# Later places for retention values, operand halves, squares and residual loads in a one-core decoder trunk

## The chip, the cores and the metric

The kernel runs on one core of a Trainium2 chip. Its five engines work side by side and wait for each other by semaphores: TensorE (PE, matmuls into PSUM), VectorE (DVE), ScalarE (ACT), GpSimd (POOL) and SyncE (SP, which here only issues transfers). The metric is the device time of one execution in microseconds (us); lower is better.

## The reference

One layer of a decoder trunk on 16 + 256 tokens of width 2048, in float32:

```python
u = rmsnorm(h, attn_norm) * vmask
aq, ak, av, rq, rk, rv, rg = split(u @ w_in)
ya = rmsnorm(diff_attention(aq, ak, av, lam, slopes, valid), attn_subln) * (1 - lam_init)
yr = rmsnorm(retention(rq, rk, rv, log_g), ret_norm) * silu(rg)
h = h + concat([ya, yr]) @ w_out
u = rmsnorm(h, ffn_norm) * vmask
h = h + (silu(causal_conv3(u @ w_gate)) * (u @ w_up)) @ w_down
out = rmsnorm(h, final_norm)[:, CHUNK:]
```

There are 8 attention heads (each with two 64-wide halves of q and k, whose softmaxes are subtracted) and 4 retention heads (128-wide q and k, 256-wide v, a decay matrix in the place of the softmax).

## The kernel before

**Precision.** Each float32 operand is split into a high part (`whi`, `xhi`, `fhi`: a cast on ACT) and a low part (`wlo`, `xlo`, `flo`: source minus high part, on DVE). A product takes three matmuls: high by high, high by low, low by high.

**Weights.** All weights stream from HBM in chunks of 128x2048 (1 MB, `raw`), loaded by `load` on SP's queue. Each chunk gives two halves of 128x1024, split by `prep`, whose inner function `halves` issues the cast and the subtraction (lines 204 and 205). `ahead(hf)` issues loads some halves ahead and splits two halves ahead (three in the last stage).

**Stages.** First the input projection, 48 units: each `gemm` (lines 434 to 436) runs 16 k-steps of three matmuls into one PSUM tile. Units 0 to 23 are q, k, v of the eight attention heads; then come q, k and two v units of each retention head and two gate units each, in the order `RSEQ`. Then the output projection (16 units), gate and up projections (88 units), and the down projection.

**The side queue.** All else in the first stages is put as small tasks into the list `side`. `pump(n)` runs n of them, every fourth k-step, so a place of the list is 4 x 3 = 12 matmuls. `att_tasks` gives an attention head's tasks (scores, softmax, transposes, values), `ret_tasks` a retention head's: `scores`, `vtr` (loads the transposed values `rvt` back from DRAM), five empty places, `av` (the value matmuls, line 619, into `ro`), an empty place, `stats`, `scale`. The values get there by `turned`: a DVE transpose to `rvb`, four small transfers to DRAM (`rhv`), and two back (`rvt`, lines 609 and 610). A scheduler orders the instructions of each engine by these places and by its own estimate of when inputs are ready; calls under `keep` hold their order.

**Halves of q and k.** After an attention head's three units, lines 682 to 691 issue at once, for each half, two casts on ACT and three DVE operations: the low part of q into `q2`, a copy of k into `k2`, and the low part of k into `klz`.

**Down.** `down_order` lays out two groups g = 0, 1, each of two 512-wide column blocks for two row blocks (four results `o`) and helper sums (`x`). A group's entries are 20 plain ones (`w`: 12 matmuls, one split) and 12 times four parts of a Strassen-like product (`d`, `u`, `t`, `c`: 6, 6, 6 and 3 matmuls, four splits and one more subtraction). `LEAD[g]` sets how many plain entries open and close it; the others are spread between the parts. The last `HOLD` = 6 entries of group 1 are held for the very end. When a group's last part is done, side tasks join the helper sums to the residual (`joined`), add the results (`take`), and square and weigh them for the final norm (`finish`: a square on ACT, line 878, and a product with the norm's weights on DVE, line 884). The residual `htok` comes back from DRAM by two loads on SP's queue at entries 20 and 28 of group 0 (line 977).

Of the kernel before, what the change touches and what calls it, by code (L numbers as in the profile page):

```python
# [2 lines left out]

# [1 line left out]

# [5 lines left out]
F32 = mybir.dt.float32  # L11
# [4 lines left out]
ALU = mybir.AluOpType  # L16
# [30 lines left out]
NS = 12  # L47
KP = 2 * NS
NPL = (NF - KP) // 2
LEAD = [(4, 3), (0, HOLD + 3)]  # L50
PARTS = ("d", "u", "t", "c")
ROOMS = (0, 1, "2a", "2b", "3a", "3b")
RSEQ = [("y", 0), ("g", 0), ("y", 1), ("g", 1), ("y", 2), ("y", 3), ("g", 2), ("g", 3)]
# [62 lines left out]
def trunk_kernel(ctx, tc, a, out):  # L116
# [73 lines left out]
    def prep(hf):  # L190
        c, s = entries[hf]
        held = len(entries) - 1 - hf
        if held < 2:
            hi, lo = [big.tile([P, 1024], F32R, tag=f"act{2 + held}{i}", name=f"end{held}{i}")
                      for i in "ab"]
        elif c >= nw and (hf - 2 * nw) % 4 == 3:
            wx = big.tile([P, 2 * 1024], F32R, tag="act0", name=f"wx{hf}")
            hi, lo = wx[:, :1024], wx[:, 1024:]
        else:
            hi = wp.tile([P, 1024], F32R, tag="whi", bufs=3, name=f"whi{hf}")  # L200
            lo = wp.tile([P, 1024], F32R, tag="wlo", bufs=3, name=f"wlo{hf}")

        def halves(src, b, e):
            S.copy(out=hi[:, b:e], in_=src)  # L204
            V.tensor_tensor(out=lo[:, b:e], in0=src, in1=hi[:, b:e].bitcast(F32),  # L205
                            op=ALU.subtract)

        if c in mixed:
            g, p = divmod(mixed[c], NS)
            if s == "d":  # L210
                halves(raw[c][:, :2 * NW], 0, 2 * NW)
            elif s == "u":
                halves(raw[c][:, 2 * NW:], 0, 2 * NW)
                two = raw[c][:, :2 * NW].rearrange("p (a c) -> p a c", a=2)
                t2 = raw[c][:, 2 * NW:3 * NW].unsqueeze(1).to_broadcast([P, 2, NW])
                V.tensor_tensor(out=two, in0=two, in1=t2, op=ALU.subtract)
            elif s == "t":
                halves(raw[c][:, :2 * NW], 0, 2 * NW)
            else:
                halves(pools["sw"][g, p], 0, NW)  # L220
        else:
            halves(raw[c][:, s * 1024:(s + 1) * 1024], 0, 1024)
        pairs[hf] = (hi, lo)
        if s in (1, PARTS[-1]):
            raw.pop(c)
# [234 lines left out]
    with ExitStack() as p1:  # L460
# [27 lines left out]
                    out=hv[:, d:d + 32].rearrange("(b t) f -> t b f", t=32),  # L488
                    in_=vb[i * 32:(i + 1) * 32].rearrange("t (b f) -> t b f", f=32))

        def att_tasks(h, q, k, hv):
            slope = 2.0 ** (-(h + 1))
            tasks = []
            As = {}
# [1 line left out]
            at = [ap_.tile([P, 3 - j, QT], F32, tag=f"at{j}", name=f"at{h}_{j}")  # L496
                  for j in range(3)]
            bias = ap_.tile([QT, 3, T], F32, tag="bias", bufs=1, name=f"bias{h}")

            def prelude():  # L500
                S.activation(out=bias, in_=base, func=AF.Copy, scale=slope)
# [76 lines left out]
            def values():  # L578
                av()
                while late:  # L580
                    late.pop()()
                late.append(ytr)

            return [prelude, scores(0), scores(1), nop, scores(2), vload, nop, atr,
                    nop, values, nop, nop]

        def ret_tasks(r, k, q, hv):
            dt_ = ap_.tile([P, 2, NQ], F32, tag="t", name=f"dk_{r}")
# [56 lines left out]
                    V.tensor_tensor(out=t, in0=st["y"][:, c, :NQ], in1=st["r"], op=ALU.mult)  # L645
                    yn[r, c] = t

            return [scores, vtr, nop, nop, nop, nop, nop, av, nop, stats, scale]

        yn = {}  # L650

# [12 lines left out]
        for h in range(AH):  # L664
            q = ap_.tile([P, NQ], F32, tag="q", name=f"q{h}")
            k = ap_.tile([P, T], F32, tag="k", name=f"k{h}")
            v = ap_.tile([P, TV], F32, tag="v", name=f"v{h}")
            nc.gpsimd.memset(v[:, T:], 0.0)
            ps = gemm(idx, xhi, xlo, Q0, NQ, 1)
            V.scalar_tensor_tensor(out=q, in0=ps[:, :NQ], scalar=0.125, in1=rq_,  # L670
                                   op0=ALU.mult, op1=ALU.mult)
            ps = gemm(idx + 1, xhi, xlo, 0, T, 1)
            V.tensor_tensor(out=k, in0=ps[:, :T], in1=rk_, op=ALU.mult)
            ps = gemm(idx + 2, xhi, xlo, 0, T, 1)
            V.tensor_tensor(out=v[:, :T], in0=ps[:, :T], in1=rk_, op=ALU.mult)
            hv = dp.tile([TV, P], F32, name=f"hv{h}")
            turned(v, ap_.tile([P, TV], F32, tag="g0", name=f"vb{h}"), hv, 0)
            idx += 3
            q2 = ap_.tile([P, 2, NQ], F32R, tag="q2", name=f"q2_{h}")
            k2 = ap_.tile([P, 2, T], F32R, tag="k2", name=f"k2_{h}")  # L680
            kl = klz[:, h % 2]
            for m in range(2):
                hs, os = slice(m * 64, m * 64 + 64), slice(64 - m * 64, 128 - m * 64)
                S.copy(out=q2[hs, m], in_=q[hs])
                V.tensor_tensor(out=q2[os, m], in0=q[hs], in1=q2[hs, m].bitcast(F32),
                                op=ALU.subtract)
                S.copy(out=k2[hs, m], in_=k[hs])
                V.tensor_copy(out=k2[os, m], in_=k[hs])
                V.tensor_tensor(out=kl[hs, m], in0=k[hs], in1=k2[hs, m].bitcast(F32),
                                op=ALU.subtract)  # L690
            side.extend(att_tasks(h, q2, (k2, kl), hv))
        for kind, r in RSEQ:
            if kind == "g":
                for c in range(2):
# [59 lines left out]
    with ExitStack() as p2:  # L754
# [156 lines left out]
        for g in range(2):  # L911
# [60 lines left out]
            held = []  # L972
            for i, (kind, x, y) in enumerate(seq):
                ahead(e)
                if not g and i in (20, 28):
                    m = (i - 20) // 8
                    keep(nc.sync.dma_start(out=htok[:, m], in_=hd[m * P:(m + 1) * P]))
                if g and i >= len(seq) - HOLD:
                    held.append((y, e))
                    e += 1  # L980
                    continue
                wt = pairs[e]
                if kind == "w":
                    for m in range(2):
                        for kk in range(2):
                            product((m, x % 2), acts(m, KP + 2 * y + kk), wt, kk * NW)
                elif y == "d":
                    product((0, 0), acts(0, 2 * x + 1), wt, 0)
                    product((0, 1), forms(x, 2), wt, NW)
                elif y == "u":  # L990
                    product(6, forms(x, 0), wt, 0)
                    product(7, forms(x, 1), wt, NW)
                elif y == "t":
                    product((1, 0), acts(1, 2 * x + 1), wt, 0)
                    product(5, acts(1, 2 * x), wt, NW)
                else:
                    product(1, acts(0, 2 * x), wt, 0)
                pairs.pop(e)
                e += 1
                if i == last_s:  # L1000
                    side.extend(joined())
                    side.extend([take(0, 0), finish(0, 0), take(1, 0), finish(1, 0)])
                    if g:
                        side.append(lambda: S.activation(out=root, in_=so[:, 1, 2:3],
                                                         func=AF.Sqrt))
                pump(3 if i > last_s else 1)
            pump(len(side))
            if not g:
                take(0, 1)()
                take(1, 1)()  # L1010
                side.extend([finish(0, 1), finish(1, 1), lambda: norm(1)])
                side.extend([nop] * 12 + [lambda: norm_scale(1)])
                continue
            po = [bank[0, 1], bank[1, 1]]
# [117 lines left out]
```

## Time and profile before

| | us |
|---|---|
| median of three runs (1162.79 to 1163.71) | 1163.69 |
| the profiled execution | 1163.84 |
| its span, first to last instruction | 1162.0 |
| TensorE busy in the span | 1144.7 |
| TensorE idle in 250 to 300 us (second and third retention head) | 4.56 |
| TensorE idle in 1150 to 1162 us (end) | 7.91 |

An instruction row of the profile has its start, its duration, the engine, the line, the operation and what it writes and reads. In brackets stands how long the engine was idle before it and what ended that. A row of the list of waits has engine, line and what was waited for, then the total in us, the number of waits and the longest. A window row has the stretch and, for each engine, its busy time and count in that stretch, then the granted clock of TensorE, the share of the DMA engines and GB/s. Matmuls are pipelined: the durations of neighbours overlap, and what a matmul costs is the distance between two starts.

### The profile page before, as it was taken

The numbers are of one execution on the slowest core, as the hardware profiler recorded it, in microseconds if no ns is written. First come the engines' busy times: TensorE is split into PE (matmuls) and PEld (weight loads), VectorE is DVE, ScalarE is ACT, GpSimd is POOL, SyncE is SP. The second block draws the span as 40 slices with busy tenths as digits, with TensorE's granted clock in tenths as the row PEclk, the third lists the DMA queues.
The fourth block names the chain that finished last, engine by engine and source line by source line (L and its number), as shares of the span: only waits on it lengthen the run. The fifth ranks groups of instructions, "written<-read, shape, count | busy, mean of one in ns | idle before, by whom it ended". The sixth has DMA issues, their size and how long they took to land.

```text
span 1162.0 us, 20666 instructions
## 1 busy us (share of the span) xinstructions
PE 1144.7 (99%) x7967; PEld 1069.8 (92%) x7967; DVE 931.5 (80%) x1737; ACT 604.0 (52%) x996; POOL 36.2 (3%) x84
## 2 busy tenths in 40 slices
PE   9999999989999999999999999999999999999997
PEld 8999999989999999999999999999999988887886
DVE  7888887657577778888888888788787778899896
ACT  7566665433245444545444544444444455666663
POOL 0000000000000000000000000000000000000000
PEclk9999999999999999999999999999999999999999
DMA  8544545564547776776777677787786589869871
GB/s 306 200 165 159 168 153 189 172 212 156 159 166 235 230 228 207 254 272 240 270 283 257 246 278 267 274 299 267 278 281 238 210 297 373 287 251 333 299 283 72
DMA packets 94914, 276.37 MB, mean 238 GB/s; under 512 B 43490, under 2 KB 51082, under 8 KB 73056
## 3 DMA queue, kind: packets, MB, share of 16 engines
q1 hardware_dynamic: 86512, 237.69, 59.3%
q0 software_dynamic: 8160, 37.23, 8.6%
q8 instruction: 62, 1.02, 0.3%
q14 instruction: 36, 0.29, 0.1%
q10 hardware_dynamic: 144, 0.14, 0.1%
HBM read 251.17 MB, written 23.86 MB: 237 GB/s over the span
## 4 chain that ended last, share of the span: by engine, by line
PE 92%; DMA 5%; DVE 2%; issue 0%; SPq 0%; ACT 0%; DVEq 0%; ACTq 0%
PE mm L455 14%; PE mm L444 10%; PE mm L442 10%; PE mm L443 10%; PE mm L457 7%; PE mm L435 7%; PE mm L434 7%; PE mm L436 7%; PE o L857 4%; PE o L858 4%; PE o L859 4%; PE x L857 2%; PE x L859 2%; PE x L858 2%; DMA rvt<-rhv 1%; DMA raw<-in_w_first_dram 1%
## 5 line engine op out<-in xcount | busy, mean ns | idle before, releaser
L204 ACT CAST whi<-raw 128x1024 fp32r<-128x1024 f32 x381 | 399.3, 1051 | 381.1 <-issue 86.7
L205 DVE TENSOR_TENSOR wlo<-raw,whi 128x1024 fp32r<-128x1024 f32 x381 | 464.7, 1223 | 139.0 <-ACT whi L204 133.8
L455 PE MATMUL mm<-g,whi 128*128 128x512 f32 x352 | 124.4, 393 | 0.0
L434 PE MATMUL mm<-x,whi 128*128 128x272 f32 (+1 forms) x344 | 101.0, 293 | 0.0
L436 PE MATMUL mm<-x,wlo 128*128 128x272 f32 (+1 forms) x344 | 99.6, 290 | 1.2 <-DVE wlo L205 1.2
L435 PE MATMUL mm<-x,whi 128*128 128x272 f32 (+1 forms) x344 | 100.0, 291 | 0.0
L444 PE MATMUL mm<-g,wlo 128*128 128x258 f32 x352 | 99.5, 283 | 0.0
L442 PE MATMUL mm<-g,whi 128*128 128x260 f32 x352 | 99.3, 282 | 0.0
L457 PE MATMUL mm<-g,wlo 128*128 128x256 f32 x352 | 98.7, 280 | 0.0
L443 PE MATMUL mm<-g,whi 128*128 128x256 f32 x352 | 97.9, 278 | 0.0
L455 PEld LDWEIGHTS mm<-g,whi 128*128 128x128 f32 x352 | 66.1, 188 | 13.0
L442 PE MATMUL mm<-ys,whi 128*128 128x260 f32 x256 | 71.9, 282 | 0.0
L444 PE MATMUL mm<-ys,wlo 128*128 128x258 f32 x256 | 71.9, 281 | 0.0
L443 PE MATMUL mm<-ys,whi 128*128 128x256 f32 x256 | 70.8, 277 | 0.0
L443 PEld LDWEIGHTS mm<-g,whi 128*128 128x128 f32 x352 | 66.7, 190 | 1.9
L436 PEld LDWEIGHTS mm<-x,wlo 128*128 128x128 f32 x344 | 65.7, 191 | 1.4 <-DVE wlo L205 1.4
L457 PEld LDWEIGHTS mm<-g,wlo 128*128 128x128 f32 x352 | 66.3, 188 | 0.0
L442 PEld LDWEIGHTS mm<-g,whi 128*128 128x128 f32 x352 | 66.1, 188 | 0.0
L444 PEld LDWEIGHTS mm<-g,wlo 128*128 128x128 f32 x352 | 66.1, 188 | 0.0
L435 PEld LDWEIGHTS mm<-x,whi 128*128 128x128 f32 x344 | 65.8, 191 | 0.1
L434 PEld LDWEIGHTS mm<-x,whi 128*128 128x128 f32 x344 | 65.8, 191 | 0.1
L858 PE MATMUL o<-wlo,fhi 128*128 128x512 f32 x158 | 61.9, 391 | 0.1
(404 smaller groups left out, 3063.2 us busy)
## 6 DMA issues: line engine op xcount, KB each, us to landing
raw<-in_w_in_dram SPq DMA_DIRECT2D x44, 1024.0 KB
raw<-in_w_gate_dram SPq DMA_DIRECT2D x44, 1024.0 KB
raw<-in_w_up_dram SPq DMA_DIRECT2D x44, 1024.0 KB
raw<-in_w_down_dram SPq DMA_DIRECT2D x20, 1024.0 KB
ts<-in_w_mix_dram POOLq DMA_DIRECT2D x24, 768.0 KB, 5.9
raw<-in_w_out_dram SPq DMA_DIRECT2D x16, 1024.0 KB
td<-ts POOLq DMA_DIRECT2D x24, 512.0 KB, 4.5
raw<-in_w_mix_dram SPq DMA_DIRECT2D x24, 512.0 KB
```

The source lines that it names most:

```text
L204: S.copy(out=hi[:, b:e], in_=src)
L205: V.tensor_tensor(out=lo[:, b:e], in0=src, in1=hi[:, b:e].bitcast(F32), op=ALU.subtract)
L434: PE.matmul(ps[:, :n], wh, xh, start=(k == 0), stop=False)
L435: PE.matmul(ps[:, :n], wh, xl, start=False, stop=False)
L436: PE.matmul(ps[:, :n], wl, xh, start=False, stop=(k == KT - 1))
L442: PE.matmul(ps[:, :NQ + 2], wh, src.cols(k, GO - 2, GL), start=(k == 0), stop=False)
L443: PE.matmul(ps[:, 4:NQ + 2], wh, src.cols(k, GL, GW), start=False, stop=False)
L444: PE.matmul(ps[:, 2:NQ + 2], wl, src.hi(k), start=False, stop=(k == KT - 1))
L455: PE.matmul(ps, wh, src.cols(k, GO + 2, GW), start=(k == 0), stop=(k == KT - 1))
L457: PE.matmul(ps[:, :SEQ], wl, src.cols(k, GO + 2, GL), start=False, stop=False)
L857: PE.matmul(o, ah, wh, start=start, stop=False)
L858: PE.matmul(o, ah, wl, start=False, stop=False)
```

## The change

The value matmuls of retention heads 0 to 2 stand two places later in the side queue (`av`, and with it `stats` and `scale`); head 3 keeps its places. The halves of q and k become a task of their own, `parted`, at the head of an attention head's list, one place after the head's units; one empty place at the list's end goes. Within it the DVE operations of one half now stand together, and for heads 0 and 1 they are kept in order. The splits of halves 9 to 15 are issued with high priority. In down, group 1 opens with two plain entries instead of none and closes with one less; the squares and weighings of group 0's first column block move from that group's end into group 1, with those of the second block; the residual loads go from entries 20 and 28 to 40 and 48.

```diff
-LEAD = [(4, 3), (0, HOLD + 3)]
+LEAD = [(4, 3), (2, HOLD + 2)]
 def halves(src, b, e):
-    S.copy(out=hi[:, b:e], in_=src)
-    V.tensor_tensor(out=lo[:, b:e], in0=src, in1=hi[:, b:e].bitcast(F32),
-                    op=ALU.subtract)
+    with tc.high_priority() if 8 < hf < 16 else nullcontext():
+        S.copy(out=hi[:, b:e], in_=src)
+        V.tensor_tensor(out=lo[:, b:e], in0=src, in1=hi[:, b:e].bitcast(F32),
+                        op=ALU.subtract)
...
+def parted():
+    pin = keep if h < 2 else (lambda ins: ins)
+    for m in range(2):
+        hs, os = slice(m * 64, m * 64 + 64), slice(64 - m * 64, 128 - m * 64)
+        S.copy(out=q[hs, m], in_=qf[hs])
+        pin(V.tensor_tensor(out=q[os, m], in0=qf[hs], in1=q[hs, m].bitcast(F32),
+                            op=ALU.subtract))
+        S.copy(out=k[0][hs, m], in_=kf[hs])
+        pin(V.tensor_copy(out=k[0][os, m], in_=kf[hs]))
+        pin(V.tensor_tensor(out=k[1][hs, m], in0=kf[hs],
+                            in1=k[0][hs, m].bitcast(F32), op=ALU.subtract))
...
-return [prelude, scores(0), scores(1), nop, scores(2), vload, nop, atr,
-        nop, values, nop, nop]
+return [parted, prelude, scores(0), scores(1), nop, scores(2), vload, nop, atr,
+        nop, values, nop]
...
-return [scores, vtr, nop, nop, nop, nop, nop, av, nop, stats, scale]
+return [scores, vtr, *[nop] * (7 if r < RH - 1 else 5), av, nop, stats, scale]
...
-if not g and i in (20, 28):
-    m = (i - 20) // 8
+if not g and i in (40, 48):
+    m = (i - 40) // 8
     keep(nc.sync.dma_start(out=htok[:, m], in_=hd[m * P:(m + 1) * P]))
...
 if i == last_s:
     side.extend(joined())
-    side.extend([take(0, 0), finish(0, 0), take(1, 0), finish(1, 0)])
+    side.extend([take(0, 0), take(1, 0)])
     if g:
+        side.extend([finish(0, 0), finish(1, 0)])
         side.append(lambda: S.activation(out=root, in_=so[:, 1, 2:3], func=AF.Sqrt))
...
 if not g:
     take(0, 1)()
     take(1, 1)()
-    side.extend([finish(0, 1), finish(1, 1), lambda: norm(1)])
+    side.extend([finish(m, j) for m, j in ((0, 0), (1, 0), (0, 1), (1, 1))])
+    side.append(lambda: norm(1))
```

The instructions of an engine stand as follows (numbers behind names are buffers; the changed program's lines are shifted by 1 to 13). TensorE at the second retention head's values, before; `mm` is the first unit of the third head, `ro` the values, `sd` the decayed scores:

```order
L436 MATMUL mm_3636<-x_69,wlo_3566 128x272
L619 MATMUL ro_3621<-sd_0_3485,rvt_3488 128x258
L434 MATMUL mm_3636<-x_69,whi_3565 128x272
L435 MATMUL mm_3636<-x_70,whi_3565 128x272
L619 MATMUL ro_3621<-sd_1_3486,rvt_3488 128x172
L619 MATMUL ro_3621<-sd_2_3487,rvt_3488 128x86
```

and with the change, at the end of the same unit's first eight k-steps:

```order
L436 MATMUL mm_3625<-x_70,whi_3565 128x272
L437 MATMUL mm_3625<-x_69,wlo_3566 128x272
L632 MATMUL ro_3656<-sd_0_3485,rvt_3488 128x258
L632 MATMUL ro_3656<-sd_1_3486,rvt_3488 128x172
L632 MATMUL ro_3656<-sd_2_3487,rvt_3488 128x86
```

The same three come once more, for the other half of the values, before the unit goes on.
From this head's score matmuls to its first value matmul stand 93 unit matmuls before and 108 now; for the first head it is 58 and 82, for the third 84 and 108, for the last 84 and 84. The two unit matmuls that stood inside the group are gone from it.

VectorE after the first four units, before; `q`, `k`, `v` with `mm` are the units' results taken from PSUM, `q_0`, `k_0`, `klz` the halves of the first head, `q_1`, `k_1` of the second, `wlo_656` and `wlo_719` low halves of the weights of units 6 and 7:

```order
L685 TENSOR_TENSOR q_0_484<-q_470,q_0_484 64x258
L688 CAST k_1_694<-k_504 64x272 x2
L205 TENSOR_TENSOR wlo_656<-raw_416,whi_655 128x1024
L689 TENSOR_TENSOR klz<-k_471,k_0_485 64x272 x2
L685 TENSOR_TENSOR q_1_693<-q_503,q_1_693 64x258
L675 TENSOR_TENSOR v_505<-mm_606,rstd_88 128x272
L685 TENSOR_TENSOR q_1_693<-q_503,q_1_693 64x258
L689 TENSOR_TENSOR klz<-k_504,k_1_694 64x272 x2
L205 TENSOR_TENSOR wlo_719<-raw_607,whi_718 128x1024
```

Ahead of the first `wlo` stand the halves of the first head but its `klz` rows, and the copies of k of the second; the rest of both stands between the two `wlo`. With the change:

```order
L509 CAST k_0_485<-k_471 64x272
L485 STREAM_TRANSPOSE vb_478<-v_472 128x288
L206 TENSOR_TENSOR wlo_638<-raw_416,whi_637 128x1024
L510 TENSOR_TENSOR klz<-k_471,k_0_485 64x272
L506 TENSOR_TENSOR q_0_484<-q_470,q_0_484 64x258
L509 CAST k_0_485<-k_471 64x272
L510 TENSOR_TENSOR klz<-k_471,k_0_485 64x272
L688 TENSOR_TENSOR v_495<-mm_588,rstd_88 128x272
L206 TENSOR_TENSOR wlo_709<-raw_589,whi_708 128x1024
```

The second head's halves have left this stretch; they stand three splits later. The first `wlo` stands behind one q half and one k cast of the first head, where two of each and two k casts of the second head stood.

ScalarE around the change of group in down, before; `whi`, `wx` are high halves of weights, `sq` the squares of the first group:

```order
L204 CAST whi_12264<-raw_12216 128x1024
L204 CAST whi_12292<-raw_12216 128x1024
L204 CAST whi_12315<-raw_12216 128x1024
L204 CAST wx_12340<-sw_0_12218 128x512
L878 ACTIVATE sq_0_12282,so<-htok_11416 128x512
L878 ACTIVATE sq_0_12310,so<-htok_11417 128x512
L204 CAST whi_12352<-raw_12285 128x1024
L878 ACTIVATE sq_1_12349,so<-htok_11416 128x512
L204 CAST whi_12365<-raw_12313 128x1024
L204 CAST whi_12384<-raw_12285 128x1024
L878 ACTIVATE sq_1_12362,so<-htok_11417 128x512
```

and with the change:

```order
L205 CAST whi_12266<-raw_12216 128x1024
L205 CAST whi_12285<-raw_12216 128x1024
L205 CAST whi_12301<-raw_12238 128x1024
L882 ACTIVATE sq_0_12349,so<-htok_11416 128x512
L205 CAST wx_12333<-raw_12238 128x1024
L882 ACTIVATE sq_0_12370,so<-htok_11417 128x512
L882 ACTIVATE sq_1_12383,so<-htok_11416 128x512
L205 CAST whi_12354<-raw_12238 128x1024
L205 CAST whi_12373<-sw_0_12240 128x512
L882 ACTIVATE sq_1_12396,so<-htok_11417 128x512
```

The first two casts of the changed list are group 1's plain entries (`raw_12216`), which stood among its parts before; `whi_12301` and `wx_12333` are its first `d` and `u` parts. Counted from group 1's first cast, the squares stand at places 5, 6, 8 and 11 before and 4, 6, 7 and 10 now, against parts that begin two entries later.

More of the change, by code (lines that the diff above doesn't have):

```diff
@@ L1 @@
 import math
-from contextlib import ExitStack
+from contextlib import ExitStack, nullcontext
 import numpy as np
@@ L489, in turned, with att_tasks @@
                     in_=vb[i * 32:(i + 1) * 32].rearrange("t (b f) -> t b f", f=32))
-        def att_tasks(h, q, k, hv):
+        def att_tasks(h, qf, kf, q, k, hv):
             slope = 2.0 ** (-(h + 1))
@@ L681, in trunk_kernel @@
             kl = klz[:, h % 2]
[L682 to L691, printed above, removed]
+            side.extend(att_tasks(h, q, k, q2, (k2, kl), hv))
         for kind, r in RSEQ:
```

## Prediction

> **What bounds the kernel now.** I read the page first, then TensorE's list of waits, then windows and the timeline around each wait.
>
> ```profile
> span 1162.0 us, 20666 instructions
> PE 1144.7 (99%) x7967; PEld 1069.8 (92%) x7967; DVE 931.5 (80%) x1737; ACT 604.0 (52%) x996; POOL 36.2 (3%) x84
> PE ro L619 <- DMA rvt<-rhv: 5.0, 2, 3.0
> ...
> PE mm L436 <- DVE wlo L205: 1.2, 1, 1.2
> PE psx L436 <- DVE wlo L205: 0.5, 1, 0.5
> ```
>
> TensorE (PE) is busy for 99%. No edit takes a matmul away, so the change can only return what PE loses between matmuls. That is 1162.0 - 1144.7 = 17.3 us of idle time, plus what hides inside "busy". The waits that the change can reach are three: 5.0 us for the transposed retention values (`rvt`, in two waits), 1.2 and 0.5 us for a low half of weights (`wlo`) near the start. The rest of the idle time lies at the first loads and behind the last matmul, where nothing is moved.
>
> Two things hide inside "busy". The first is the clock.
>
> ```profile
> 254.33 0.29 PE L434 MATMUL mm<-x,whi 128*128 128x272 f32 x1
> ...
> 255.32 0.29 PE L436 MATMUL mm<-x,wlo 128*128 128x272 f32 x1
> ...
> 259.34 2.41 PE L619 MATMUL ro<-sd,rvt 86*128 86x172 f32 x10 [3.04 <-DMA rvt<-rhv]
> 300.47 2.58 PE L619 MATMUL ro<-sd,rvt 86*128 86x172 f32 x10 [1.99 <-DMA rvt<-rhv]
> 51.84 0.39 PE L436 MATMUL mm<-x,wlo 128*128 128x272 f32 x1 [1.20 <-DVE wlo L205]
> 260.00:262.00 2.00, 2.00 (x9) 1.87 (x9) 0.00 (x0) 0.21 (x1) 0.00 (x0) 0.54 0.07 29
> 262.00:264.00 2.00, 2.00 (x12) 2.00 (x11) 0.86 (x2) 0.86 (x3) 0.00 (x0) 0.61 0.00 0
> 300.00:302.00 2.00, 1.53 (x7) 1.35 (x8) 0.26 (x1) 0.00 (x0) 0.00 (x0) 0.78 0.78 328
> 302.00:304.00 2.00, 2.00 (x10) 2.00 (x9) 0.22 (x1) 0.66 (x2) 0.00 (x0) 0.50 0.12 49
> 304.00:306.00 2.00, 2.00 (x16) 2.00 (x15) 0.63 (x2) 0.41 (x1) 0.00 (x0) 0.87 0.03 12
> 51.00:52.00 1.00, 0.16 (x1) 0.17 (x2) 1.00 (x2) 0.35 (x1) 0.00 (x0) 1.00 0.82 321
> ```
>
> In a window row the first seven columns are the stretch, its length and the busy time of PE, of weight loads, of VectorE (DVE), ScalarE (ACT) and POOL; then come the granted clock, the DMA share and GB/s. Behind the 3.04 us wait the clock was 0.54 and 0.61, which loses 2 x 0.46 + 2 x 0.39 = 1.70 us; behind the 1.99 us wait it was 0.78, 0.50 and 0.87, which loses 0.44 + 1.00 + 0.26 = 1.70 us. Both stretches count as busy. Behind the 1.20 us wait the clock stayed at 1.00. So a retention wait costs itself and 1.7 us more; the early one costs only itself.
>
> The second is matmuls that start late without the record showing a gap.
>
> ```profile
> 950.00:1000.00 50.00, 49.79 (x219) 40.63 (x218) 43.36 (x41) 30.12 (x33) 0.00 (x0) 1.00 0.92 342
> 1000.00:1050.00 50.00, 49.79 (x216) 39.88 (x215) 44.88 (x50) 30.33 (x40) 0.00 (x0) 1.00 0.71 259
> 1050.00:1100.00 50.00, 50.00 (x221) 40.94 (x220) 46.15 (x44) 31.10 (x34) 0.54 (x1) 1.00 0.89 313
> ```
>
> These are three stretches of the down projection, with one mix of 512-wide matmuls. The full one holds 221 matmuls, 50 / 221 = 0.226 us each. The stretch with the residual loads holds 219 and that with the change of group 216: 2 x 0.226 = 0.45 and 5 x 0.226 = 1.13 us are lost, though each shows 0.21 us idle. The Trainium skill ("Perfetto Trace Analysis", Identifying the Most-Contended Engine) says why busy time is no measure here: pipelined matmuls hide it, and the busy share of weight loads tells more. Those rows agree (40.63 and 39.88 against 40.94). By busy time this term would be 0.4 us, and the sum below 0.6 us later at most.
>
> **Part 1, retention values two places on.** For heads 0 to 2 the six value matmuls, and with them the statistics and the scaling behind them, move by two places of the side queue; a place is 12 matmuls. For the third head (the wait of 1.99 us) the order shows 24 matmuls more ahead of them. The nine matmuls from 254.33 to 255.32 start 0.99 / 8 = 0.124 us apart, so 24 are about 3 us: the wait goes, with 1 us to spare, and its 1.70 us of slow clock with it. For the second head the order shows only 15 more, since two of the old place's matmuls already stood inside the group: the second value matmul comes 13 x 0.124 = 1.61 us later, and 3.04 - 1.61 = 1.43 us of wait stays, if the copy lands when it did.
>
> ```profile
> 248.02 0.35 SPq L185 DMA_DIRECT2D raw<-in_w_in_dram  x1
> 250.67 8.62 DMA rvt<-rhv
> 292.63 7.80 DMA rvt<-rhv
> ```
>
> The copy's chain is untouched: it begins with the last value unit on PE, and a weight load of 1 MB is still issued just ahead of it (248.02). Landing took 8.62 us there and 7.80 us a head later. The remaining wait is bounded by 0 (a copy 1.4 us earlier; the other head's was 0.8 earlier) and 3.04 (one later by as much); I take 1.43. Does it halve the clock again? 1.20 us did not, 1.99 us did; 1.43 is nearer to 1.20, and I take no, keeping 1.70 us as the other end. The last head keeps its place and has no wait. The later statistics hold their PSUM buffer 3 us longer; its next user is the next head's values, which move as well.
>
> Gain: 1.99 + 1.61 + 2 x 1.70 = 7.0 us.
>
> **The clock and the skill.** The Trainium skill ("TensorE: Matmul & The Clock Gate", What's actually happening) says that the clock halves after an idle window of about 3.4 us, counted freely. The rows above agree on the length of the slow stretch and differ on its cause: 1.99 us idle was enough. By the page alone the remaining 1.43 us would leave the clock alone, as I took it; neither old wait would have cost any clock either, and the sum would be 9.7 - 3.4 = 6.3 us.
>
> **Part 2, halves of q and k one place later.** The work is the same, 4 casts on ACT and 6 operations on DVE a head. It moves behind the `wlo` that PE waits for.
>
> ```profile
> 46.17 1.23 DVE L205 TENSOR_TENSOR wlo<-raw,whi 128x1024 fp32r<-128x1024 f32 x1
> 47.31 0.90 DVE L689 TENSOR_TENSOR klz<-k,k 64x272 fp32r<-64x272 f32 x2
> ...
> 49.62 0.91 DVE L689 TENSOR_TENSOR klz<-k,k 64x272 fp32r<-64x272 f32 x2
> 50.56 1.23 DVE L205 TENSOR_TENSOR wlo<-raw,whi 128x1024 fp32r<-128x1024 f32 x1
> 46.56 2.00 ACT L204 CAST whi<-raw 128x1024 fp32r<-128x1024 f32 x2
> ```
>
> In the new order a q half (0.45) and three k casts (0.9) leave the way to the first `wlo`, which then starts near 44.8 instead of 46.17; PE waited 0.5 us for it. Behind it come 2.1 us of work instead of 3.1, so the second `wlo` starts near 48 instead of 50.56, just after its high half (the first of the two casts from 46.56). It ends near 49.2, and PE would want it at 51.84 - 1.20 - 0.5, about 50.1. Both waits go: 1.7 us. The cover is 1 us; without it 1.2 us come back. The deferred halves of the second head (2.4 us) then stand ahead of its first scores, and of a `wlo` that PE wants some 3 us later. Bounds: 1.7 gained, and a new wait of 1.2.
>
> **Part 3, down.** The four squares and weighings of the first group leave its end, where squares stand ahead of a cast of weights.
>
> ```profile
> 1041.09 0.63 ACT L878 ACTIVATE sq<-htok 128x512 f32<-128x512 f32 x1
> ...
> 1042.61 1.05 ACT L204 CAST whi<-raw 128x1024 fp32r<-128x1024 f32 x1
> 1029.92 0.69 DVE L908 TENSOR_TENSOR htok<-x,htok 128x512 f32<-128x512 f32 x1
> 974.23 0.32 SPq L977 DMA_DIRECT2D htok<-hd  x1
> fn<-in_final_norm_dram POOLq DMA_DIRECT2D x2, 512.0 KB, 6.3
> 1147.78 0.69 DVE L1023 TENSOR_TENSOR htok<-o,htok 128x512 f32<-128x512 f32 x1 [3.59 <-PE o L859]
> ```
>
> The second group opens with two plain entries of 12 matmuls, 5.4 us of PE for two splits of about 1.2 us, where it opened with split-heavy parts. But four weighings of 0.6 us on DVE now fall on the parts behind them, so I take 1.0 us of the 1.6 found above. Bounds: all 1.6 gained, and 0.5 lost (what the residual loads cost now, paid again at their new place). The second half of the final norm's weights goes, on POOL's queue, into the buffer that these weighings read, so its load (6.3 us) starts later by as much as they do; its scaling stands some 18 DVE operations behind them, and nothing else waits for it before the tail. The residual loads move 20 entries down SP's queue. The second was issued at 974.23; 20 entries of 3 to 12 matmuls, 6.7 on average, take 20 x 6.7 x 0.226 = 30 us, so it goes out near 1004, 25 us before the first add on the residual (1029.92). The tail has one plain entry (2.7 us) less between the last squares and the end, against 3.59 us of DVE idle ahead of the last add: hidden.
>
> **The sum.** 7.0 + 1.7 + 1.0 = 9.7 us off this execution's 1163.84 us (span 1162.0 and 1.8 around it; the median of the three runs, 1163.69, is 0.15 less): **1154.1 us**.
>
> **The rivals.**
>
> ```profile
> 60.00:100.00 40.00, 40.00 (x341) 40.00 (x340) 35.95 (x129) 28.41 (x75) 0.22 (x2) 1.00 0.50 165
> 1030.00:1040.00 10.00, 10.00 (x46) 8.29 (x45) 10.00 (x14) 3.81 (x5) 0.00 (x0) 1.00 0.66 241
> ```
>
> - The remaining 1.43 us halves the clock after all: 1155.8. For it, 1.99 us did; against it, 1.20 us did not. 15%.
> - The copy lands early and no retention wait is left: 1152.7. The 7.80 us landing speaks for it, an untouched chain against. 10%.
> - The order does not do in the early stage and in down what it says (other operations stand ahead of `wlo`, the squares only move the loss): 1154.1 + 1.7 + 1.0 = 1156.8. For it, DVE is busy for 10.00 of 10 us ahead of the change of group; against it, the new order's rows. 15%.
> - The slow clock comes without the waits: 1154.1 + 3.4 = 1157.5. Against it, both slow stretches begin within 2 us of a wait's end. 3%. The Trainium skill's page on the clock gate, named above, allows it, since by its rule both waits were too short.
> - The deferred halves make a `wlo` late by 1.2 us, as at 51.84, but at every one of eight heads: 9.6 us, and with one clock loss of 1.7 us 1165.4, **slower**. It decides from about 1.2 us a head; DVE is busy for 35.95 of 40 us from 60 us on, which speaks for it, and TensorE for 40.00, which speaks against. 5%. At four to five heads it ends within the noise, near 1161.8 to 1163: 7%.
>
> **How the numbers follow.** The forecast has 45%. The range takes the early copy and both full gains in down at its low end, 1152.3, and at its high end the third rival with a clock loss on it, 1158.5; what lies outside is the 12% of the last rival and a little below. About 0.2% (2.3 us) is what a measurement of this kernel can tell from no change, so faster means under 1161.4: 45 + 15 + 10 + 15 + 3 = 88%; within it 7%; slower 5%.
>
> **What would show it.** Right: TensorE's list of waits holds one wait for `rvt` of about 1.4 us and no `wlo` wait under 60 us; the granted clock is 1.00 through the retention heads; 220 or 221 matmuls in each 50 us of down. Wrong: a clock row of 0.5 near the second head's values, a `wlo` wait between 60 and 200 us, or a window of down with 217 or fewer.

## The result and the profile after

| | before | with the change |
|---|---|---|
| median of four runs each (us) | 1163.24 (1160.98 to 1163.71) | 1156.24 (1155.66 to 1157.24) |
| the profiled execution | 1163.84 | 1155.66 |
| its span | 1162.0 | 1153.8 |

The ratio is 0.9945, with an interval of 0.9927 to 0.9962: 6.4 us faster, 4.4 to 8.5. The forecast was 9.7 us, to 1154.1. The page of the changed kernel, its first lines and TensorE's list of waits:

```profile
span 1153.8 us, 20661 instructions
PE 1139.7 (99%) x7967; PEld 1066.6 (92%) x7967; DVE 931.0 (81%) x1737; ACT 604.7 (52%) x996; POOL 36.4 (3%) x84
...
PE ro L632 <- DMA rvt<-rhv: 1.4, 1, 1.4
PE mm L333 <- ACT whi L325: 1.2, 2, 1.0
PE o L861 <- ACT wx L205: 1.2, 1, 1.2
PE x L861 <- ACT whi L205: 0.5, 1, 0.5
```

One wait for `rvt` is left, of the 1.4 us that the prediction gave it, and both early `wlo` waits are gone. New are 1.2 us at the first loads (0.4 before) and two waits in down, 1.2 us for a `wx` and 0.5 for a `whi`. The windows say the same: first the two of the retention heads, then those of down.

```profile
250.00:300.00 50.00, 48.62 (x385) 47.93 (x384) 31.06 (x51) 18.94 (x24) 0.00 (x0) 1.00 0.55 174
300.00:350.00 50.00, 50.00 (x411) 49.77 (x410) 39.12 (x76) 21.72 (x33) 0.00 (x0) 1.00 0.55 183
...
950.00:1000.00 50.00, 50.00 (x223) 41.39 (x222) 43.95 (x41) 31.09 (x34) 0.00 (x0) 1.00 0.89 313
1000.00:1050.00 50.00, 48.31 (x212) 39.19 (x211) 43.11 (x48) 28.71 (x36) 0.54 (x1) 1.00 0.74 282
1050.00:1100.00 50.00, 49.92 (x220) 40.79 (x219) 45.57 (x44) 30.82 (x35) 0.00 (x0) 1.00 0.88 309
```

In the retention heads the clock is 1.00 (0.97 and 0.97 before). In down the first window gained (223 matmuls, 219 before) and the second lost (212, 216 before). So the signs that the prediction named point both ways: one `rvt` wait of 1.4 us, no early `wlo` wait and a clock of 1.00 were its signs of being right; a window of down with 217 matmuls or fewer was one of being wrong, and here is one with 212.

**A ledger.** Busy time hides late matmuls, so I numbered the matmuls of projections and down in program order and took the start of one number in both traces. Five of them, before (the last line stands in the tail):

```profile
36.64 0.28 PE L435 MATMUL mm<-x3b,whi 128*128 128x272 f32 x1
70.31 0.29 PE L435 MATMUL mm<-x3b,whi 128*128 128x258 f32 x1
333.39 0.28 PE L434 MATMUL mm<-x2a,whi 128*128 128x258 f32 x1
982.33 0.39 PE L859 MATMUL o<-whi,flo 128*128 128x512 f32 x1
1153.33 0.28 PE L858 MATMUL oe<-end0b,fhi 128*128 128x256 f32 x1
```

and with the change:

```profile
37.65 0.28 PE L436 MATMUL mm<-x3b,whi 128*128 128x272 f32 x1
69.07 0.29 PE L436 MATMUL mm<-x3b,whi 128*128 128x258 f32 x1
324.73 0.28 PE L435 MATMUL mm<-x2a,whi 128*128 128x258 f32 x1
973.64 0.39 PE L863 MATMUL o<-whi,flo 128*128 128x512 f32 x1
1145.17 0.28 PE L862 MATMUL oe<-end0b,fhi 128*128 128x256 f32 x1
```

The start was 1.01 us later (37.65 - 36.64), the next stretch gave back 2.25 (69.07 - 70.31 = -1.24), attention and retention together 7.42 (-8.66), and down from there on lost 0.5 (-8.69 to -8.16). The table does this for every kernel of the study, each by one profiled execution: us against the profiled execution of before, lost (+) or gained (-), in each stretch (in times of before).

| kernel | start, to 37 | early, to 70 | attention, to 255 | retention, to 333 | down to 982 | 982 to 990 | 990 to 1024 | 1024 to 1107 | sum |
|---|---|---|---|---|---|---|---|---|---|
| the change | +1.01 | -2.25 | -0.16 | -7.26 | -0.03 | -0.68 | +1.52 | -0.30 | -8.16 |
| ret_only | -0.48 | +0.32 | -0.06 | -3.01 | +0.03 | -0.69 | 0.00 | -0.01 | -3.90 |
| early_only | -0.12 | -2.25 | -0.11 | -2.48 | +0.04 | -0.69 | 0.00 | -0.03 | -5.64 |
| down_only | -0.22 | +0.16 | -0.01 | -2.25 | 0.00 | -0.69 | +1.06 | -0.32 | -2.29 |
| res_back | +0.13 | -2.25 | -0.16 | -7.42 | +0.01 | -0.69 | 0.00 | -1.45 | -11.85 |
| res_pool | +0.65 | -2.25 | -0.16 | -5.77 | +2.28 | -0.69 | 0.00 | -1.29 | -7.24 |
| ret_8 | +0.07 | -2.25 | -0.16 | -8.25 | -0.02 | -0.17 | 0.00 | -0.91 | -11.71 |
| lead_alone | +1.15 | -2.25 | -0.16 | -7.04 | +0.07 | -0.05 | 0.00 | -0.81 | -9.11 |
| squares_alone | +0.29 | -2.25 | -0.16 | -7.20 | 0.00 | -0.69 | 0.00 | +0.06 | -9.95 |
| r8_res4048 | +1.41 | -1.76 | -0.16 | -7.66 | -0.02 | -0.69 | +0.94 | -0.34 | -8.29 |
| r8_res4149 | +1.09 | -2.25 | -0.16 | -8.11 | -0.02 | -0.70 | +0.01 | -1.44 | -11.59 |
| r8_act | +0.27 | -2.15 | -0.16 | -7.55 | -0.02 | -0.69 | +1.68 | -0.86 | -9.49 |
| r8_nopin | +0.29 | +1.45 | -0.34 | -8.54 | 0.00 | -0.68 | +0.01 | -1.45 | -9.27 |

Read by columns, it separates the edits from chance. The start goes from -0.48 to +1.41 whatever the kernel: the changed kernel's +1.01 is no part of its edits. The 0.69 us at 982 to 990 us is gained by kernels that change nothing in down (`ret_only`, `early_only`): the profiled execution of before lost it, and not every execution does. What it is comes below, with the residual loads.

### The profile page after: what moved, and what is told of

Its sections match the earlier page's. It is cut to its first block, busy times and chain, and to the rows that moved or that the text cites. A ratio compares the mean times of both kernels' runs of the same rounds, so it can differ in the third digit from the quotient of the medians.

```text
span 1153.8 us, 20661 instructions
## 1 busy us (share of the span) xinstructions
PE 1139.7 (99%) x7967; PEld 1066.6 (92%) x7967; DVE 931.0 (81%) x1737; ACT 604.7 (52%) x996; POOL 36.4 (3%) x84
## 4 chain that ended last, share of the span: by engine, by line
PE 95%; DMA 3%; DVE 1%; ACT 0%; SPq 0%; issue 0%; DVEq 0%; ACTq 0%
PE mm L456 14%; PE mm L445 10%; PE mm L443 10%; PE mm L444 10%; PE mm L435 7%; PE mm L436 7%; PE mm L458 7%; PE mm L437 7%; PE o L861 4%; PE o L862 4%; PE o L863 4%; PE x L861 2%; PE x L863 2%; PE x L862 2%; DMA raw<-in_w_down_dram 1%; PE po L575 1%
## 5 line engine op out<-in xcount | busy, mean ns | idle before, releaser
L435 PE MATMUL mm<-x,whi 128*128 128x272 f32 (+1 forms) x344 | 99.5, 289 | 0.0
L436 PE MATMUL mm<-x,whi 128*128 128x272 f32 (+1 forms) x344 | 98.9, 288 | 0.0
L862 PE MATMUL o<-wlo,fhi 128*128 128x512 f32 x149 | 58.0, 390 | 0.0
```

Source lines behind the costliest of these rows:

```text
L435: PE.matmul(ps[:, :n], wh, xh, start=(k == 0), stop=False)
L436: PE.matmul(ps[:, :n], wh, xl, start=False, stop=False)
L862: PE.matmul(o, ah, wl, start=False, stop=False)
```

## The experiments

Times are medians; the ratio is to runs of before on the same chip, whose medians in the three groups were 1162.65, 1163.3 and 1162.9 us.

| kernel | median (lowest to highest) | ratio and interval |
|---|---|---|
| ret_only | 1157.61 (1155.81 to 1159.94) | 0.9956, 0.9944 to 0.9969 |
| early_only | 1159.54 (1158.19 to 1162.03) | 0.9975, 0.9966 to 0.9984 |
| down_only | 1164.70 (1161.53 to 1166.32) | 1.0013, 1.0004 to 1.0022 |
| res_back | 1153.90 (1152.01 to 1155.19) | 0.9922, 0.9909 to 0.9936 |
| res_pool | 1155.96 (1155.01 to 1160.60) | 0.9944, 0.9925 to 0.9963 |
| ret_8 | 1152.01 (1151.62 to 1152.29) | 0.9908, 0.9892 to 0.9924 |
| lead_alone | 1154.62 (1153.05 to 1155.64) | 0.9929, 0.9911 to 0.9947 |
| squares_alone | 1155.75 (1153.86 to 1158.11) | 0.9941, 0.9920 to 0.9962 |
| r8_res4048 | 1152.72 (1152.02 to 1155.52) | 0.9909, 0.9890 to 0.9929 |
| r8_res4149 | 1152.11 (1151.57 to 1153.26) | 0.9901, 0.9884 to 0.9918 |
| r8_act | 1152.32 (1152.24 to 1154.55) | 0.9906, 0.9888 to 0.9924 |
| r8_nopin | 1154.56 (1153.23 to 1155.49) | 0.9921, 0.9903 to 0.9939 |

### One part alone: ret_only, early_only, down_only

Each is the kernel before with the lines of one part: `ret_only` the list of `ret_tasks`; `early_only` `parted` with the priority and the kept order; `down_only` `LEAD`, `finish` and the loads of `htok`.

> Only the retention values move two places on; the halves, the squares, the opening and the residual loads stand as before. Theory: the two waits for rvt fall from 3.04 and 1.99 us to one of about 1.4, and both slow stretches of the clock (1.70 us each) go: 7.0 us, so 1156.2 against 1163.2, no loss elsewhere, and a granted clock of 1.00 in 250 to 306 us. Rival A: the clock counts in free-running windows, and a wait of 1.4 us that falls badly halves it too; then some executions lie 1.7 us higher, near 1158. Rival B: part of the gain seen behind the second head came from the early stage; then less than 6 us.

> Only the halves of q and k become a task of their own (with the priority of splits 9 to 15 and the kept order of the first two heads). Theory: the two wlo waits of 0.49 and 1.20 us go and nothing else changes: 1.7 to 2.2 us, so about 1161.3 against 1163.2. Rival: the start, 1.0 us later in the changed kernel's profile, is this part's doing; then 1.2 us net, about 1162.0, and the first matmuls of unit 0 again wait 1.0 us for whi.

> Only the down projection changes: opening of group 1, squares and weighings, residual loads at entries 40 and 48. The prediction gave 1.0 us of gain (1162.2). The changed kernel's profile reads as 0.5 us of loss (1163.7): about 0.7 us gained where the residual loads went from, 1.5 lost where they went to (a wait of 1.2 for a high half whose weights landed late), 0.5 gained at the change of group, 0.2 lost later. Rival: that wait came from the shift of time by the other parts; then there is no wait of 1.2 us here and up to 1 us of gain.

By the ratios the three are worth -5.1 us (1162.65 x 0.0044; 3.6 to 6.5), -2.9 (1.9 to 4.0) and +1.5 (0.5 to 2.6). Their sum, -6.5, is what the whole change measured (-6.4): the parts add up within their intervals, and down is the one that costs. `early_only` gave more than its 1.7 to 2.2, and its start is not later in the ledger (-0.12), so its rival falls. `down_only`'s rival falls too: in its profile PE waits 0.77 us, at 1014.03 us, for a `wx` whose weights came late, though no other part shifts the time there.

`ret_only` fell short of its 7.0. In its profile, the slowest of its five executions, the copy landed late, PE waited 2.45 us at the second head, and the clock stayed low for longer than before. The wait's row and the windows behind it:

```profile
260.16 3.13 PE L619 MATMUL ro<-sd,rvt 86*128 86x172 f32 x10 [2.45 <-DMA rvt<-rhv]
...
260.00:262.00 2.00, 1.84 (x6) 1.75 (x7) 0.00 (x0) 0.00 (x0) 0.00 (x0) 0.56 0.66 221
262.00:264.00 2.00, 2.00 (x9) 1.91 (x9) 0.00 (x0) 0.66 (x2) 0.00 (x0) 0.50 0.82 344
264.00:266.00 2.00, 2.00 (x11) 2.00 (x10) 0.86 (x2) 0.41 (x1) 0.00 (x0) 0.50 0.01 4
266.00:268.00 2.00, 2.00 (x14) 2.00 (x13) 0.00 (x0) 0.00 (x0) 0.00 (x0) 0.74 0.00 0
```

The four rows lose 2 x (0.44 + 0.50 + 0.50 + 0.26) = 3.4 us, two slow stretches of 1.70. `down_only`, whose retention heads are those of before, gained 2.25 us there: its third head waited 1.40 us and kept the clock, where before's profiled execution waited 1.99 and lost it. So both the wait and what it costs vary from run to run, which also shows in `ret_only`'s executions, 1155.81 to 1159.94. That is near its rival A, though this wait was longer than the 1.4 us that A spoke of.

### Where the loss in down comes from: res_back, res_pool

```
res_back:  if not g and i in (20, 28):   # the loads where they were before
res_pool:  keep(nc.gpsimd.dma_start(out=htok[:, m], ...))   # at 40 and 48
```

> The changed kernel with the two residual loads back at entries 20 and 28 of down. Theory: the wait of 1.2 us for the high half near 1008 us goes and the old loss of 0.7 us comes back: 0.8 us faster than the changed kernel, about 1155.4 where that had 1156.2. Rival: the weights land late there whatever the residual loads do; then the wait stays and the time is the changed kernel's or 0.7 us above it.

> The changed kernel with its two residual loads, still at entries 40 and 48, on POOL's queue in the place of SP's. In the changed kernel's chain the second load (issued at 994.83) stands on SP's queue just ahead of a 1 MB weight load (995.20) that lands 11.8 us later, and PE waits 1.2 us for its high half. Theory A, the place on the queue: the weight load goes out 0.4 us earlier and is not behind the residual, the wait of 1.2 us shrinks below 0.5 and about 1 us is gained, near 1155. Theory B, bandwidth (the DMA share is 1.00 from 1000 to 1020 us): the residual's bytes collide wherever they are issued, the wait stays near 1.2 us and the time near the changed kernel's 1156.2.

`res_back` beats the whole change (1153.90 against 1156.24), and its ledger has no loss from 990 to 1024 us and gains 1.45 behind that. The residual loads' new place is what cost. The gain of 2.3 us is more than the 0.8 that was expected, and the old loss did not come back in this execution. The changed kernel shows how the new place costs: the queue's rows, the cast that waits, and PE.

```profile
994.83 0.32 SPq L981 DMA_DIRECT2D htok<-hd  x1
995.20 0.60 SPq L185 DMA_DIRECT2D raw<-in_w_down_dram  x1
...
1007.03 1.04 ACT L205 CAST wx<-raw 128x1024 fp32r<-128x1024 f32 x1 [1.30 <-DMA raw<-in_w_down_dram]
1008.13 0.73 PE L861 MATMUL o<-wx,fhi 128*128 128x512 f32 x2 [1.23 <-ACT wx L205]
```

The second residual load (994.83) went out just ahead of a load of down's weights (995.20). These were there 11.8 us later, ACT waited 1.30 us for them and PE 1.23 for ACT. In `res_back`, with no residual load near, the same weights are there 8.88 us after their issue:

```profile
993.65 0.43 SPq L185 DMA_DIRECT2D raw<-in_w_down_dram  x1
1002.53 1.05 ACT L205 CAST wx<-raw 128x1024 fp32r<-128x1024 f32 x1 [0.30 <-DMA raw<-in_w_down_dram]
```

The old place had the same fault, in a milder form. Before, too, the second residual load (974.23, shown in the prediction) goes out just ahead of a load of down's weights, and these are there 10.77 us later:

```profile
974.60 0.42 SPq L185 DMA_DIRECT2D raw<-in_w_down_dram  x1
985.37 2.00 ACT L204 CAST whi<-raw 128x1024 fp32r<-128x1024 f32 x2 [3.60 <-DMA raw<-in_w_down_dram]
987.42 0.50 PE L857 MATMUL o<-whi,fhi 128*128 128x512 f32 x1 [0.21 <-ACT whi L204]
```

That is the loss of 0.69 us at 982 to 990 us. Of the eight profiles with the loads at 20 and 28, seven have ACT waiting for these weights: PE lost nothing where they were there 9.16 to 10.06 us after their issue, and 0.5 to 0.7 us where it took 10.57 to 10.80 (before, `lead_alone`, `ret_8`). In the six profiles with the loads elsewhere ACT does not wait there.

`res_pool` tells less than it was meant to. POOL has nothing else to do, so it issued both loads at the very start of down, at 925.64, not at entry 40; the loss moved with them (+2.28 us by 982, none at 990 to 1024).

```profile
925.64 1.05 POOL L981 DMA_DIRECT2D htok<-hd  x2
940.54 1.04 ACT L205 CAST whi<-raw 128x1024 fp32r<-128x1024 f32 x1 [5.08 <-DMA raw<-td]
```

Of its two theories neither is decided by it. That the residual's bytes can cost at another place too fits the cast that waited 5.08 us for weights there; it is one profile.

### One place more: ret_8

`res_back` with eight empty places for the second retention head:

```
return [scores, vtr, *[nop] * ((7, 8, 7, 5)[r]), av, nop, stats, scale]
```

> The changed kernel with the residual loads back at 20 and 28, and the second retention head's values one place (12 matmuls, 1.49 us) later still. Theory: the wait that is left there, 1.2 to 1.4 us in two profiles and 2.45 with a slow clock in a third, falls to zero or nearly so, and no execution has a slow clock in 250 to 306 us: 1.2 to 1.5 us faster than the same kernel without it (1153.9), so 1152.5, and a narrower spread of its runs. Rival: the values then hold up the statistics or the next unit, and nothing is gained.

No wait for `rvt` is left in its profile, and its median is 1.9 us under that of `res_back` (1.6 by the ratios), where 1.2 to 1.5 was expected. Its four runs lie within 0.7 us. It is the fastest median of the study, 0.9908 of before (`r8_res4149` has 0.9901); the changed kernel had 0.9945. Of the four kernels below with the same places, three still have waits for `rvt`, of 0.32 to 0.76 us, with the clock at 1.00.

### Opening or squares: lead_alone, squares_alone

Both are `res_back` with one more edit undone: `lead_alone` puts the squares back at the end of group 0, `squares_alone` has `LEAD` as before.

> The changed kernel with the residual loads back at 20 and 28 and the squares and weighings of group 0's first column block back at that group's end; of the edits in down only the two plain entries at the opening of group 1 are left. With both edits the profile gained 1.45 us at the change of group against before. Theory: the plain opening gives the greater part, 1 us or more (PE has 24 matmuls for two splits), so at most 0.5 us slower than with both, 1154.4. Rival: the squares do it; then the loss at the change of group is back, near 1155.3.

> The changed kernel with the residual loads back at 20 and 28 and group 1 opening with no plain entry, as before; of the edits in down only the later squares and weighings are left. Theory: they give the smaller part, under 0.5 us of the 1.45, so about 1155.0; the stretch of the change of group again holds 4 to 5 matmuls too few. Rival: the squares give it all; then 1153.9.

From 1024 to 1066 us, around the change of group, `lead_alone` gained 1.64 us and `res_back` 1.63; `squares_alone` lost 0.06. The plain opening does all of it, the later squares nothing. (From 1066 to 1107 `lead_alone` lost 0.83 and `res_back` 0.18; `ret_8`, which has the later squares, lost 0.73, so this is not their doing.) These are single profiles; by the medians `lead_alone` is 0.7 us and `squares_alone` 1.9 us slower than `res_back`, which agrees in order, with intervals of about 2 us on each ratio.

### Ahead of the weights or behind: r8_res4048, r8_res4149, r8_act

All three have `ret_8`'s retention places. The residual loads stand at 40 and 48 as in the change, at 41 and 49, or at 40 and 48 on ScalarE's queue:

```
r8_res4149:  if not g and i in (41, 49):
r8_act:      keep(nc.scalar.dma_start(out=htok[:, m], ...))
```

> The changed kernel with only the second retention head's values one place later still (no retention wait is left, so its runs scatter little); the residual loads stay at entries 40 and 48. It is the control of the next two, and against ret_8 (same but for loads at 20 and 28, 1152.0) it gives the price of the loads' new place. Theory from the profiles: 1.0 to 1.5 us at about 1002 to 1017 and 1.1 more at the change of group, so 1154.3. Rival: the price was tied to the slow executions; then it is within 0.5 us of ret_8.

> The same with the residual loads at entries 41 and 49: on SP's queue the second one now stands behind the 1 MB load of down's weights that it stood ahead of, and nothing else moves there. Theory A, the place on the queue: the wait for the high half of these weights near 1008 us goes and about 1 us is gained against r8_res4048. Theory B, bandwidth: the residual's bytes take the DMA engines in the same microseconds, the next loads come late in their turn, and the time is the same within 0.5 us.

> The kernel r8_res4048 with its residual loads, at the same entries, issued by ScalarE between two casts and so on another queue than the weights. Theory A: as r8_res4149, about 1 us faster than r8_res4048. Theory B: the same within 0.5 us, the DMA share again 1.00 for 20 us after 1000 us.

The control lost 0.94 us from 990 to 1024, `r8_res4149` nothing, `r8_act` 1.68. In `r8_res4149` the weights go first on the same queue:

```profile
993.89 0.42 SPq L185 DMA_DIRECT2D raw<-in_w_down_dram  x1
994.53 0.51 SPq L981 DMA_DIRECT2D htok<-hd  x1
1002.84 1.06 ACT L205 CAST wx<-raw 128x1024 fp32r<-128x1024 f32 x1 [0.38 <-DMA raw<-in_w_down_dram]
```

and in `r8_act` too, with the residual 2.7 us behind on another queue:

```profile
993.73 0.42 SPq L185 DMA_DIRECT2D raw<-in_w_down_dram  x1
996.42 0.33 ACTq L981 DMA_DIRECT2D htok<-hd  x1
1004.87 1.04 ACT L205 CAST wx<-raw 128x1024 fp32r<-128x1024 f32 x1 [2.57 <-DMA raw<-in_w_down_dram]
1005.97 0.50 PE L861 MATMUL o<-wx,fhi 128*128 128x512 f32 x1 [1.36 <-ACT wx L205]
```

The weights took 8.95 us (993.89 to 1002.84) with the residual behind them on one queue, 11.14 with it on another, 11.8 in the changed kernel with it ahead (11.23 in the control, 11.37 in `down_only`), and 8.88 in `res_back` with none near. So neither theory holds as stated: the engines are shared (B), and a place behind on the same queue is what protects a load from it (A); another queue does not. The Trainium skill ("DMA: Bandwidth & Descriptors", Queues, rings and completion order) states that an engine takes turns between the queues that have work for it, a packet at a time, and works off one queue in order. The 8.95 and 11.14 us agree with it, by one profile each.

The control also gained only 0.34 us from 1024 to 1107 where `r8_res4149` gained 1.44. There the two programs differ in TensorE's order: the scheduler, with the loads one entry on or on ScalarE's queue, puts a different set of matmuls at the opening of group 1. The control has the changed kernel's order, and with it PE waits for a `whi` at 1043 us (0.46 us in the changed kernel, 0.44 here). `r8_act` has the order of `r8_res4149`, and from 1024 to 1066 it gained the full 1.62. That makes 1.1 us of the loads' price in the profiles an effect of the order, not of the bytes.

In the medians the three differ by less than their intervals: 1152.72, 1152.11, 1152.32. Against `ret_8`, the same but for loads at 20 and 28, the control is 0.7 us slower by the medians and 0.1 by the ratios, where 2.3 was forecast; its rival (within 0.5 us) is as near. The profiled executions of the control (1155.52) and of `r8_act` (1154.55, the others 1152.24 to 1152.34) were the slowest of their four, so the losses in these two profiles are not those of a typical run. Without `ret_8`'s places the same move costs 2.3 us (the change against `res_back`). What the place costs in a typical run stays open; the profiles show how it can cost.

### Place or kept order: r8_nopin

`ret_8` without the kept order of the halves:

```
pin = lambda ins: ins
```

> The kernel ret_8 without the kept order of VectorE's operations on the halves of the first two heads; their task stands where the change put it. In VectorE's order the halves then fall back to where they stood before the change, ahead of both wlo. Theory: the kept order, not the task's place, is what frees the two wlo, so the waits of 0.5 and 1.2 us are back and the kernel is 2.2 us slower than ret_8, 1154.2. Rival: the place in the list does it; then 1152.0.

Its median is 2.55 us above that of `ret_8` (1.5 by the ratios), its early stretch 3.7 us worse in the ledger (+1.45 against -2.25), and one long `wlo` wait is back. This one also halves the clock:

```profile
52.05 0.39 PE L437 MATMUL mm<-x,wlo 128*128 128x272 f32 x1 [1.88 <-DVE wlo L206]
52.00:54.00 2.00, 1.95 (x13) 1.96 (x14) 2.00 (x4) 0.00 (x0) 0.11 (x1) 0.85 0.35 80
54.00:56.00 2.00, 2.00 (x11) 2.00 (x10) 0.95 (x1) 0.00 (x0) 0.00 (x0) 0.50 0.74 110
56.00:58.00 2.00, 2.00 (x17) 2.00 (x16) 0.77 (x1) 1.83 (x2) 0.00 (x0) 0.80 0.82 328
```

The wait is 1.88 us of the 3.7, the clock 2 x (0.15 + 0.50 + 0.20) = 1.70; before's wait of 1.20 us there left the clock alone. In its program the halves stand on VectorE almost row for row where they stood before the change, though `parted` is in its new place. Without the kept order the new place gains nothing. The kept order at the old place, and the priority of the splits, which `r8_nopin` still has, were not run by themselves.

## Why the prediction was near, and where it was off

The time lay in the range; the sum of 9.7 us was 3.3 too large by the ratio. Measured one by one, part 1 gave 1.9 us less than its term, part 2 1.2 more and part 3 2.5 less, so a surplus hid some of the two misses, and that was luck. The prediction's other sum, 6.3 us without any loss of clock, is near by luck too: the profile of before did lose the clock behind both waits, and it was down that took gain away. Two small sums do not close: both full gains in down on an early copy give 1152.1, not 1152.3, and 1161.8 to 1163 belongs to five or six heads, not four or five. Point by point:

**The waits of part 1.** Right. The third head's wait went, and the second's was predicted at 1.43 us and measured 1.38. In the profiled execution the term of 7.0 us came out as 7.26.

**The clock of part 1.** Mis-sized: 2 x 1.70 us was taken from one execution in which both waits lost the clock. Over many runs the part is worth 5.1 us, not 7.0, since before does not always lose it (`down_only`'s third head) and the change does not always keep it (`ret_only`). And the step "1.43 is nearer to 1.20, and I take no" rests on a rule that is not there. Two waits of one kind, first `res_pool`'s, then `lead_alone`'s:

```profile
257.53 1.78 PE L632 MATMUL ro<-sd,rvt 86*128 86x172 f32 x10 [1.36 <-DMA rvt<-rhv]
258.00:260.00 2.00, 2.00 (x13) 1.95 (x12) 0.00 (x1) 0.66 (x2) 0.00 (x0) 0.75 0.51 111
260.00:262.00 2.00, 2.00 (x11) 2.00 (x10) 0.86 (x2) 0.42 (x2) 0.00 (x0) 0.50 0.98 406
262.00:264.00 2.00, 2.00 (x17) 2.00 (x17) 0.16 (x1) 0.24 (x1) 0.00 (x0) 0.89 0.11 41
```

```profile
258.27 1.70 PE L632 MATMUL ro<-sd,rvt 86*128 86x172 f32 x10 [1.60 <-DMA rvt<-rhv]
260.00:262.00 2.00, 2.00 (x18) 2.00 (x18) 0.83 (x2) 1.07 (x3) 0.00 (x0) 1.00 0.87 352
262.00:264.00 2.00, 2.00 (x18) 2.00 (x18) 0.47 (x2) 1.04 (x1) 0.00 (x0) 1.00 0.29 123
```

1.36 us lost 1.72 us of clock, 1.60 us lost none. Length alone does not decide. The traces' own records of the clock, finer than these rows, show what else counts. In all fourteen profiles every change of the clock lies on a grid of 3.41 us; before, for example, it is at half for 3.41 us from 260.16 and from 301.12 us on, 40.96 us or 12 steps apart. On this grid a step ended within `lead_alone`'s wait, with 1.06 us of it on one side and 0.54 on the other, while `res_pool`'s 1.36 us lay whole in one step, and at its end the clock fell. That is a window that runs freely, as the Trainium skill has it ("TensorE: Matmul & The Clock Gate", What's actually happening); the page asks for a whole idle window of about 3.4 us, and 1.36 us of idle was enough here. The place on the grid is not all either: `squares_alone`'s 1.43 us lay whole in one step too and cost nothing. What share of a window must be idle stays open.

**Part 2.** Right in what goes, low in size: 1.7 us forecast, 2.25 in the ledger of eight of the ten kernels with the kept order, so 0.55 us more had hidden in matmuls that started late without a recorded gap (`early_only`'s runs give 2.9, 1.9 to 4.0). The cause was misplaced. The heading was "halves of q and k one place later"; `r8_nopin` shows that the halves stay behind the `wlo` only with the kept order, and that the place without it gives nothing. The deferred halves made no `wlo` late in attention (-0.16 us), so the slower rival did not come.

**Part 3.** Wrong in sign: 1.0 us of gain forecast, 0.5 to 2.6 of loss measured. The step that failed is the bound on the residual loads' new place, "0.5 lost": in the profiles it cost 0.9 to 1.5 us for weights that land late, and 1.1 more through another order of matmuls at the opening of group 1. I had worked out when the residual would be wanted, not which load would stand behind it. The loss at the old place was read rightly but taken as one of every run: 0.45 us forecast, 0.69 in this execution, nothing in five of the eight profiles with the loads there. The opening held: `res_back` gained the 1.45 us that the plain opening was to bring, between the 1.0 taken and the bound of 1.6; but the squares, which the prediction put first, had no part in it that the ledger shows.

**What was not in the sum.** The start, which scatters by 1.9 us between profiles.

## What to carry to other kernels

A load moved to "a later place" has to be read against the load behind it on its queue: put it behind the one whose data are due next, not ahead, and not on another queue in the same microseconds. Price a clock loss or a stall only when more than one execution shows it; the matmuls of two traces, numbered in program order, show where a gain or a loss lies. A loss that only some executions have may still have one cause, as at the residual loads' old place: look what the engine waited for before calling it chance. Where a scheduler sets the order, look whether the place or the kept order made the difference before moving the place again.

## What was not expected of the hardware

Waits of 1.20, 1.38, 1.40, 1.43 and 1.60 us left TensorE's clock at 1.00; one of 1.36 us halved it for 3.41 us, as did one of 1.88, and one of 2.45 us for twice as long. All changes of the clock lie on a grid of 3.41 us within an execution. And a 1 MB load shared the DMA engines with one issued 2.7 us later on another queue (11.14 us to be read), while one 0.64 us behind it on its own queue left it ahead (8.95 us, against 8.88 with none near).
